# Other queues for the stores, other places in memory and another order at two seams of a diffusion layer

## The chip, the cores and the metric

The kernel runs on one core of a Trainium2 chip. Its engines are TensorE (PE, matmuls), VectorE (DVE), ScalarE (ACT), GpSimd (POOL) and SyncE (SP), which here only issues DMAs. Each engine runs its own instructions in order, and waits on semaphores for the others. The metric is the device time of one execution in microseconds (us), lower is better; three runs of the kernel before gave a median of 2388.57 (2385.91 to 2389.51).

## The reference

One layer over 2048 tokens of width 1024 with 256 context tokens: a bidirectional gated linear attention (GLA) and a SwiGLU with hidden width 2816, each between two RMS norms and modulated by a conditioning vector. Cut to what is run:

```python
h_lat = modulate(rms_norm(lat, g0), m0, m1)
y_lat, _ = gla_mixer(h_lat, h_ctx, ...)        # chunk scans in both directions, head norm, silu(r), w_out
lat = lat + m2 * rms_norm(y_lat, g1)
h = modulate(rms_norm(lat, g2), m3, m4)
gate, up = jnp.split(h @ ffn_w_in, 2, axis=-1)
lat = lat + m5 * rms_norm((jax.nn.silu(gate) * up) @ ffn_w_out, g3)
```

## The kernel before

All matmuls are done in three passes on split operands (`hi` is rounded to fp32r, `lo` is the rest: hi x hi, hi x lo, lo x hi). The program is written as stages, and a scheduler of the framework puts each engine's instructions in an order of its own; what it may do is set by the memory pools. A pool takes a place on the left or right side of SBUF or PSUM, its tiles have a number of buffers (`bufs`), and a tile of a later pool that lies over an earlier one waits for that pool's close and for the tiles there (`reuse_waits="tile"`).

The first stage makes the projections, gates and the chunks' scores. The second is the back pass (`back`, L654 to 757): chunk after chunk, from 15 to 0, the state E is taken along, `o` is formed (L695), normed (`on`, L703, by POOL's `rh`), gated and transposed, and projected by `wo` (`py`, L739, whose squares ACT sums). With POOL's `ry` DVE scales it (L751), adds the residual `xt` (L753, on POOL but for the last chunk), SP stores the sum `l1_d` (`l_d` in the trace, L754), and a norm (`xh`, L93 and L95, by POOL's `rb`) follows. `mh`, `my`, `mb` and `sst` are the small sums ahead of `rh`, `ry` and `rb`.

SwiGLU's input is the modulated transpose of `xh` (L102/103). It is multiplied by a seven-product scheme of the Strassen kind: each half `p` of the tokens needs seven operands T_d[p][P1..P7]. Two are the transposes of a group of 512 tokens (`first`); the other five come from the other group (`second`, L771 to 787): two loads `bl`, two transposes `hf`, four differences (L781) and their stores. POOL forms them for the group that comes first, DVE for the last group (group 0), whose units stand as `pend` behind the back pass. Each T is loaded and split by `load_T` (L855 to 863) into a pool that is partly (`hR`) only opened when the back pass's right side (`p2t`) has closed.

SwiGLU (L897 to 990) runs 44 features, 2 halves of the tokens by 22 pieces. `Feat.product(i)` splits a weight block (`whl`, L933/934) and does twelve matmuls of 128x512 into X, Y or Z; the products come in the order `CHAIN`, P1, P2, P6, P7, P5, P4, P3. The results `a` are stored, with differences `sa`, into S_d; sums of the second weight matrix (`wl`) are stored into W_d in between. The last stage (`out_group`) multiplies S_d by W_d or the weights through rings `ar`, `wr` and `wraw` (L1026 to 1039), fourteen deep, and ends with a norm (L1052 to 1056). All stores are issued by SP (`st` is `nc.sync`).

Of the kernel before, what the change touches and what calls it, by code (L numbers as in the profile page):

```python
# [15 lines left out]
D = 1024  # L16
# [3 lines left out]
H = 4  # L20
# [14 lines left out]
def trunk(ctx, tc, x, cx, modw, cols, rows, consts, wqkr, wv, wvg, wgate, wout, w1, w2, out):  # L35
# [17 lines left out]
    qb_d = [dram.tile([128, H, 128], F32, name=f"qb_d{c}") for c in range(NC_)]  # L53

# [12 lines left out]
    pT = ExitStack()  # L67
    tbp = pT.enter_context(tc.tile_pool(name="tbp", bufs=1))
    Tb = tbp.tile([128, H, DV], F32, name="Tb")
# [105 lines left out]
    Tf = gp.tile([128, H, DV], F32, name="Tf")  # L175
    glt = [c1.tile([128, 128], F32R, name=f"glt{i}") for i in range(4)]
# [177 lines left out]
    def gla_stages(g, i, c, first):  # L354
# [279 lines left out]
    p2t = ExitStack()  # L634
    sp = p2.enter_context(tc.tile_pool(name="sp", bufs=2, reuse_waits="tile"))
# [14 lines left out]
    def back(gc):  # L650
# [13 lines left out]
        def b0():  # L664
# [10 lines left out]
            if gc == NC_ - 1:  # L675
                E[0] = sp.tile([128, H, DV], F32, name="E", tag="E", bufs=3)
                for h in range(H):
                    nc.scalar.activation(out=E[0][:, h, :], in_=Tb[:, h, :], func=AF.Copy, scale=fb[:, gc, h:h + 1])
# [50 lines left out]
        def b3(n):  # L729
            ohi, olo = e["o"]  # L730
            if n == 0:
                e["y"] = sq.tile([128, D], F32, name="y2", tag="y2", bufs=2)
# [9 lines left out]
        def b4(xhs):  # L742
# [11 lines left out]
            st.dma_start(out=l1_d[gc], in_=y)  # L754
# [4 lines left out]
    def h2_units(g, xhs):  # L759
# [3 lines left out]
        def hmod(k):  # L763
            hf = sq.tile([128, GT], F32, name="hf2", tag="hf2", bufs=4)
# [6 lines left out]
        def second(k):  # L771
# [6 lines left out]
            st.dma_start(out=Td[P3][k], in_=b22)  # L778

            def comb(i, out, x, y):  # L780
                eng.tensor_tensor(out=out, in0=x, in1=y, op=ALU.subtract)  # L781
                st.dma_start(out=Td[i][k], in_=out)
# [3 lines left out]
            t2 = sq.tile([128, GT], F32, name="t2", tag="hf2", bufs=4)  # L786
# [5 lines left out]
        return [lambda k=k: second(k) for k in range(4)]  # L792

# [29 lines left out]
    for i, gc in enumerate(order):  # L823
# [12 lines left out]
        if gc % 4 == 0:  # L836
            pend += h2_units(gc // 4, xhs[gc // 4][::-1])
    p2.close()
    pT.close()
# [3 lines left out]
    p3 = ExitStack()  # L843
    hL = p3.enter_context(tc.tile_pool(name="hL", bufs=1, reuse_waits="tile"))
    w3 = p3.enter_context(tc.tile_pool(name="w3", bufs=2, reuse_waits="tile"))
    o3 = p3.enter_context(tc.tile_pool(name="o3", bufs=2, reuse_waits="tile"))
    ps3 = p3.enter_context(tc.tile_pool(name="ps3", bufs=1, space=PSUM, reuse_waits="tile"))
    for u in pend:
        u()
    p2t.close()  # L850
    hR = p3.enter_context(tc.tile_pool(name="hR", bufs=1, reuse_waits="tile", side="right"))
    ps3z = p3.enter_context(tc.tile_pool(name="ps3z", bufs=1, space=PSUM, reuse_waits="tile", side="right"))
    T = {}

# [42 lines left out]
    class Feat:  # L897
# [32 lines left out]
        def product(self, i):  # L930
# [6 lines left out]
            if i == P1:  # L937
                self.X = ps3.tile([128, GT], F32, name="X", tag="X", bufs=3)
# [56 lines left out]
    for i in CHAIN:  # L995
        load_T(1, i)
# [193 lines left out]
```

## Time and profile before

| | value |
|---|---|
| profiled execution | 2384.77 us |
| its span | 2383.0 us (1.8 around it) |
| median of three runs | 2388.57 us (2385.91 to 2389.51) |
| mean granted PE clock | 0.986 of full speed |
| busy share | PE 97%, DVE 65%, ACT 45%, POOL 8% |
| DMA | 463.98 MB, mean 195 GB/s |

The table is read so: PE's 97% is an average; 3% of the span, some 81 us, is PE idle time, and a transfer or another engine that PE waits for shows as a gap of its timeline, with what released it in brackets. In PE rows "x12" groups matmuls of one kind, and the next start minus this start is what they take. `SPq` is the DMA queue of SP: a row is the issue of a transfer, not its landing.

### The profile page before, as it was taken

Reading aid. Unit: us, or ns where it says so; the run is one execution under the profiler, and the core shown is the slowest. Engines: PE = TensorE matmul, PEld = TensorE weight load, DVE = VectorE, ACT = ScalarE, POOL = GpSimd, SP = SyncE. Lnnn points to the kernel's source line nnn. Section 1 sums busy time; section 2 is a strip of 40 time slices with the busy share of each in tenths; the row PEclk is TensorE's granted clock in tenths of the full one; section 3 lists DMA queues with packets and bytes.
Section 4 is the critical chain, followed back from the end, with each engine's and each line's share of the span. In section 5 each row is a group of like instructions: output and inputs, shape, how many; then the busy total and the mean of one; then the engine's idle time right before and its main releaser. Section 6 shows DMA issues by size and latency. Waiting matters only on the chain.

```text
span 2383.0 us, 32426 instructions
## 1 busy us (share of the span) xinstructions
PE 2302.0 (97%) x11546; PEld 1939.9 (81%) x11546; DVE 1557.7 (65%) x2478; ACT 1068.8 (45%) x1947; POOL 186.6 (8%) x274
## 2 busy tenths in 40 slices
PE   8999999999998999897999999999999989999998
PEld 4898898898898878685888888888888868888887
DVE  6756666766658576658776666866666647466554
ACT  3535445445547544335433333533333336554552
POOL 1100000000001033631000000000000000001001
PEclk9999999999999999997999999999999999999999
DMA  8765468565455587758787332633233248559655
GB/s 299 225 208 173 148 197 285 177 210 208 153 191 191 206 274 257 243 186 309 258 264 259 125 111 93 230 102 115 97 106 107 75 149 284 191 192 330 201 181 177
DMA packets 228902, 463.98 MB, mean 195 GB/s; under 512 B 22530, under 2 KB 66178, under 8 KB 228740
## 3 DMA queue, kind: packets, MB, share of 16 engines
q1 hardware_dynamic: 228740, 461.92, 57.3%
q8 instruction: 90, 1.47, 0.3%
q14 instruction: 72, 0.59, 0.1%
HBM read 331.27 MB, written 130.56 MB: 194 GB/s over the span
## 4 chain that ended last, share of the span: by engine, by line
PE 52%; DMA 0%; DVE 0%; SPq 0%; ACT 0%; issue 0%; POOLq 0%; POOL 0%; ACTq 0%
PE X L951 20%; PE Z L951 10%; PE X L1074 10%; PE W L1074 8%; PE Y L951 5%; DMA wraw<-w 0%; DMA T<-T_d 0%; DMA T_d<-hf 0%; DVE sa L984 0%; DVE bl L781 0%; DVE y L1055 0%; SPq L906 0%; DVE t L781 0%; DVE hf L781 0%; DVE a L974 0%
## 5 line engine op out<-in xcount | busy, mean ns | idle before, releaser
L951 PE MATMUL X<-T,whl 128*128 128x512 f32 x2112 | 495.7, 390 | 8.2 <-ACT whl L933 7.1
L951 PEld LDWEIGHTS X<-T,whl 128*128 128x128 f32 x2112 | 396.6, 188 | 91.5 <-ACT whl L933 7.5
L951 PE MATMUL Z<-T,whl 128*128 128x512 f32 x1056 | 256.2, 391 | 9.1 <-ACT T L861 9.1
L1074 PE MATMUL X<-wr,ar 128*128 128x512 f32 x1056 | 242.3, 391 | 10.6 <-ACT wr L1038 10.6
L1074 PEld LDWEIGHTS X<-wr,ar 128*128 128x128 f32 x1056 | 199.2, 189 | 52.8 <-ACT wr L1038 11.1
L951 PEld LDWEIGHTS Z<-T,whl 128*128 128x128 f32 x1056 | 199.3, 189 | 51.6 <-ACT T L861 9.5
L86 PE MATMUL pj<-hhi,whi 128*128 128x512 f32 (+1 forms) x544 | 213.6, 395 | 2.1 <-DVE hhi L75 1.4
L87 PE MATMUL pj<-hlo,whi 128*128 128x512 f32 (+1 forms) x544 | 211.4, 389 | 0.0
L88 PE MATMUL pj<-hhi,wlo 128*128 128x512 f32 (+1 forms) x544 | 210.4, 387 | 0.0
L73 ACT CAST whi<-wf 128x1024 fp32r<-128x1024 f32 x104 | 109.0, 1048 | 192.7 <-PE pj L87 84.4
L1028 DVE TENSOR_TENSOR ar<-ar 128x512 fp32r<-128x512 f32 x154 | 106.2, 691 | 131.1 <-ACT ar L1027 130.6
L76 DVE TENSOR_TENSOR wlo<-wf,whi 128x1024 fp32r<-128x1024 f32 x104 | 126.8, 1220 | 86.5 <-ACT whi L73 81.0
L1074 PE MATMUL W<-wr,ar 128*128 128x512 f32 x792 | 180.5, 389 | 0.0
L1074 PEld LDWEIGHTS W<-wr,ar 128*128 128x128 f32 x792 | 148.7, 188 | 30.8
L1027 ACT CAST ar<-ar 128x512 fp32r<-128x512 f32 x154 | 95.5, 621 | 154.6 <-DMA ar<-S_d 107.0
L86 PE MATMUL pj<-whi,hhi 128*128 128x256 f32 x432 | 125.0, 289 | 6.3 <-DVE gs L292 4.9
L951 PE MATMUL Y<-T,whl 128*128 128x512 f32 x528 | 127.7, 390 | 0.0
L87 PE MATMUL pj<-wlo,hhi 128*128 128x256 f32 x432 | 123.2, 285 | 2.8 <-DVE wlo L76 2.8
L88 PE MATMUL pj<-whi,hlo 128*128 128x256 f32 x432 | 122.7, 284 | 0.0
L87 PEld LDWEIGHTS pj<-hlo,whi 128*128 128x128 f32 x544 | 103.5, 190 | 21.3 <-DVE hlo L76 2.2
L86 PEld LDWEIGHTS pj<-hhi,whi 128*128 128x128 f32 x544 | 103.1, 191 | 21.5 <-DVE hhi L75 1.6
L88 PEld LDWEIGHTS pj<-hhi,wlo 128*128 128x128 f32 x544 | 103.4, 190 | 19.7
(231 smaller groups left out, 4273.7 us busy)
## 6 DMA issues: line engine op xcount, KB each, us to landing
ar<-S_d SPq DMA_DIRECT2D x154, 256.0 KB, 3.0
wf<-wqkr SPq DMA_DIRECT2D x68, 512.0 KB, 3.9
wg<-w SPq DMA_DIRECT2D x44, 512.0 KB, 3.5
wu<-w SPq DMA_DIRECT2D x88, 256.0 KB, 2.7
S_d<-sa SPq DMA_DIRECT2D x88, 256.0 KB, 2.0
wr<-W_d SPq DMA_DIRECT2D x88, 256.0 KB, 3.0
wf<-wv SPq DMA_DIRECT2D x36, 512.0 KB, 3.8
wl<-w SPq DMA_DIRECT2D x66, 256.0 KB, 3.7
```

Source lines behind the costliest of these rows:

```text
L73: nc.scalar.copy(out=hi, in_=src)
L76: nc.vector.tensor_sub(out=lo, in0=src, in1=hi.bitcast(F32))
L86: nc.tensor.matmul(out=ps, lhsT=ahi, rhs=bhi, start=start, stop=False)
L87: nc.tensor.matmul(out=ps, lhsT=ahi, rhs=blo, start=False, stop=False)
L88: nc.tensor.matmul(out=ps, lhsT=alo, rhs=bhi, start=False, stop=stop)
L951: nc.tensor.matmul(out=ps, lhsT=w[:, a, ks], rhs=t[:, k, b, :], start=first and k == 0 and n == 0, stop=k == 3 and n == 2, skip_group_chec ...
L1027: nc.scalar.copy(out=t[:, 0, :], in_=raw)
L1028: nc.vector.tensor_sub(out=t[:, 1, :], in0=raw, in1=t[:, 0, :].bitcast(F32))
L1074: nc.tensor.matmul(out=po[j], lhsT=a[:, x, 128 * j:128 * j + 128], rhs=w[:, z, :], start=first and fp == 0 and n == 0, stop=fp == NFP - 1 ...
```

## The change

Six things are changed. The stores of l1, of most operand sums, of W_d and of S_d are issued by `nc.gpsimd` (POOL) instead of SP: 250 DMA issues in all (only the P3 store for the first group stays on SP). The backward start state Tb is scaled in the first stage, stored and loaded back by a DMA, so that its memory ends early. T for P1 has a pool `hG` of its own, opened before the back pass, and is loaded when chunk 3 has been done; P2, P6, P7, P5 and P4 lie in `hL` on the left, and only P3, `wl`, `g1` and `sa` lie in `hR`. The first products are written in another order, with one unit of sums behind each of feature 0's P6, P7, P5 and P4. X has two PSUM buffers instead of three, Z one instead of two; `hf2` has three instead of four. And the last stage's rings are divided over three pools, of which `rA` (four of `ar`) and `rB` (ten of `wr`, `wraw`) lie over memory that frees early.

```diff
+                        for h in range(H):
+                            nc.scalar.activation(out=Tb[:, h, :], in_=Tb[:, h, :], func=AF.Copy, scale=fb[:, gc, h:h + 1])
+                        st.dma_start(out=Tb_d, in_=Tb.rearrange("p h v -> p (h v)"))
...
+    p3 = ExitStack()
+    hG = p3.enter_context(tc.tile_pool(name="hG", bufs=1, reuse_waits="tile"))
...
-                for h in range(H):
-                    nc.scalar.activation(out=E[0][:, h, :], in_=Tb[:, h, :], func=AF.Copy, scale=fb[:, gc, h:h + 1])
+                sync.dma_start(out=E[0].rearrange("p h v -> p (h v)"), in_=Tb_d)
...
-            st.dma_start(out=l1_d[gc], in_=y)
+            nc.gpsimd.dma_start(out=l1_d[gc], in_=y)
...
-            st.dma_start(out=Td[P3][k], in_=b22)
+            (st if g > 1 else nc.gpsimd).dma_start(out=Td[P3][k], in_=b22)
...
-                st.dma_start(out=Td[i][k], in_=out)
+                nc.gpsimd.dma_start(out=Td[i][k], in_=out)
...
-            t2 = sq.tile([128, GT], F32, name="t2", tag="hf2", bufs=4)
+            t2 = sq.tile([128, GT], F32, name="t2", tag="hf2", bufs=3)
...
+    T, T_pool = {}, {P1: hG}
+    def load_T(p, i):
+        t = T_pool[i].tile([128, 4, 2, GT], F32R, name=f"T{i}", tag=f"T{i}", bufs=1)
+        for k in range(4):
+            raw = t[:, k, 1, :].bitcast(F32)
+            sync.dma_start(out=raw, in_=T_d[p][i][k])
+            nc.scalar.copy(out=t[:, k, 0, :], in_=raw)
+            nc.vector.tensor_sub(out=t[:, k, 1, :], in0=raw, in1=t[:, k, 0, :].bitcast(F32))
+        T[i] = t
...
+        if gc == 3:
+            load_T(1, P1)
...
-    pT.close()
-    p3 = ExitStack()
+    w3 = p3.enter_context(tc.tile_pool(name="w3", bufs=2, reuse_waits="tile"))
...
-    w3 = p3.enter_context(tc.tile_pool(name="w3", bufs=2, reuse_waits="tile"))
...
-    for u in pend:
-        u()
-    p2t.close()
-    hR = p3.enter_context(tc.tile_pool(name="hR", bufs=1, reuse_waits="tile", side="right"))
-    ps3z = p3.enter_context(tc.tile_pool(name="ps3z", bufs=1, space=PSUM, reuse_waits="tile", side="right"))
-    T = {}
-    def load_T(p, i):
-        pool = hL if i in (P1, P2, P6) else hR
-        t = pool.tile([128, 4, 2, GT], F32R, name=f"T{i}", tag=f"T{i}", bufs=1)
-        for k in range(4):
-            raw = t[:, k, 1, :].bitcast(F32)
-            sync.dma_start(out=raw, in_=T_d[p][i][k])
-            nc.scalar.copy(out=t[:, k, 0, :], in_=raw)
-            nc.vector.tensor_sub(out=t[:, k, 1, :], in0=raw, in1=t[:, k, 0, :].bitcast(F32))
-        T[i] = t
+    T_pool.update({i: hL for i in (P2, P6, P7, P5, P4)})
...
-            t = o3.tile([128, 512], F32, name="wl", tag="wl", bufs=3)
+            t = hR.tile([128, 512], F32, name="wl", tag="wl", bufs=3)
...
-            st.dma_start(out=W_d[i][fp], in_=x)
+            nc.gpsimd.dma_start(out=W_d[i][fp], in_=x)
...
-                self.X = ps3.tile([128, GT], F32, name="X", tag="X", bufs=3)
+                self.X = ps3.tile([128, GT], F32, name="X", tag="X", bufs=2)
...
-                self.Z = ps3z.tile([128, GT], F32, name="Z", tag="Z", bufs=2)
+                self.Z = ps3.tile([128, GT], F32, name="Z", tag="Z", bufs=1)
...
-                g1 = o3.tile([128, GT], F32, name="g1", tag="g1", bufs=1)
+                g1 = hR.tile([128, GT], F32, name="g1", tag="g1", bufs=1)
...
-            st.dma_start(out=S_d[self.p][i][self.f % NFP], in_=t)
+            nc.gpsimd.dma_start(out=S_d[self.p][i][self.f % NFP], in_=t)
...
-                t = o3.tile([128, GT], F32, name="sa", tag="sa", bufs=3)
+                t = hR.tile([128, GT], F32, name="sa", tag="sa", bufs=3)
...
-    feats = {}
-    for i in CHAIN:
+    n = len(seq)
+    feats = {0: Feat(*seq[0]), 1: Feat(*seq[1])}
+    for i in (P2, P6, P7, P5, P4):
...
-    n = len(seq)
-    for t in range(n + 1):
+    for j, i in ((0, P1), (1, P1), (0, P2), (1, P2)):
+        feats[j].product(i)
+    for i in (P6, P7, P5, P4):
+        feats[0].product(i)
+        pend.pop(0)()
+    p2t.close()
+    hR = p3.enter_context(tc.tile_pool(name="hR", bufs=1, reuse_waits="tile", side="right"))
+    T_pool[P3] = hR
+    load_T(1, P3)
+    for j, i in ((1, P6), (0, P3), (1, P7)):
+        feats[j].product(i)
+    for _ in range(2):
+        units.pop(0)()
+    for t in range(2, n + 1):
...
-            if not 0 <= j < n:
+            if not j < n:
...
-        if t >= 2 and t % 2 == 0:
+        if t % 2 == 0:
...
-    r4 = p4.enter_context(tc.tile_pool(name="r4", bufs=1, reuse_waits="tile"))
+    rA = p4.enter_context(tc.tile_pool(name="rA", bufs=1, reuse_waits="tile"))
...
-    ps4 = p4.enter_context(tc.tile_pool(name="ps4", bufs=1, space=PSUM, reuse_waits="tile"))
+    rB = p4.enter_context(tc.tile_pool(name="rB", bufs=1, reuse_waits="tile"))
+    rC = p4.enter_context(tc.tile_pool(name="rC", bufs=1, reuse_waits="tile"))
+    ps4 = {"W": p4.enter_context(tc.tile_pool(name="ps4", bufs=1, space=PSUM, reuse_waits="tile")),
+           "X": p4.enter_context(tc.tile_pool(name="ps4x", bufs=1, space=PSUM, reuse_waits="tile", side="right"))}
+    count = {"ar": 0, "wr": 0}
+    def slot(tag):
+        i = count[tag] % 14
+        count[tag] += 1
+        first, nf = {"ar": (rA, 4), "wr": (rB, 10)}[tag]
+        pool, sfx, nb = (first, "", nf) if i < nf else (rC, "2", 14 - nf)
+        return pool.tile([128, 2, 512], F32R, name=tag, tag=tag + sfx, bufs=nb)
...
-        t = r4.tile([128, 2, 512], F32R, name=tag, tag=tag, bufs=14)
+        t = slot(tag)
```

The instructions are otherwise the same and as many. What the scheduler makes of it follows for three places.

PE at the seam from the back pass to SwiGLU, before (`py` is the last chunk's projection, the transposes `tp` are those of the last group's `xh`; T_10939 is P1's operand, T_10952 P2's, T_10965 P6's, T_10978 P7's):

```order
L88 MATMUL py<-wo_hi_8573,olo 128x512
L951 MATMUL X<-T_10939,whl 128x512 x2
L951 MATMUL Y<-T_10952,whl 128x512 x2
L951 MATMUL X<-T_10939,whl 128x512 x3
L102 MATMUL tp<-ident,xh 128x128 x24
L951 MATMUL X<-T_10939,whl 128x512 x4
L102 MATMUL tp<-ident,xh 128x128 x4
L951 MATMUL X<-T_10939,whl 128x512 x3
L951 MATMUL Y<-T_10952,whl 128x512 x4
L102 MATMUL tp<-ident,xh 128x128 x4
L951 MATMUL Y<-T_10952,whl 128x512 x6
L951 MATMUL X<-T_10965,whl 128x512 x12
```

and now (T_10487 is P1's, T_10854 P2's, T_10867 P6's, T_10880 P7's, T_10893 P5's and T_10906 P4's):

```order
L86 MATMUL py<-wo_hi_8579,olo 128x512
L951 MATMUL X<-T_10487,whl 128x512 x24
L100 MATMUL tp<-ident,xh 128x128 x24
L951 MATMUL Y<-T_10854,whl 128x512 x12
L951 MATMUL X<-T_10867,whl 128x512
L100 MATMUL tp<-ident,xh 128x128 x4
L951 MATMUL X<-T_10867,whl 128x512 x6
L951 MATMUL Y<-T_10854,whl 128x512 x12
L951 MATMUL X<-T_10867,whl 128x512 x5
L951 MATMUL Z<-T_10880,whl 128x512 x12
L951 MATMUL X<-T_10893,whl 128x512 x12
```

Both first features' P1 now stand in front of the transposes, and the products that follow come in the order in which the operands load. P3's first matmul stands 156 matmuls and 32 transposes behind `py`.

POOL in the sums of the first group, before, up to the next chunk's `rh` (`bl`, `hf` and `t` are the sums, y a chunk's residual sum):

```order
L781 TENSOR_TENSOR bl<-hf_10030,bl 128x512
L781 TENSOR_TENSOR hf_10030<-hf_10037,hf_10030 128x512
L781 TENSOR_TENSOR t_10049<-hf_10037,bl 128x512
L781 TENSOR_TENSOR bl<-bl,t_10049 128x512
L80 TENSOR_SCALAR mh<-ssh 128x4
L82 TENSOR_TENSOR rh<-mh,nhalf 128x4
L753 TENSOR_TENSOR y_9890<-y_9890,xt_10054 128x1024
L747 TENSOR_TENSOR sst<-ss_10075 128x1
```

and now:

```order
L784 TENSOR_TENSOR hf_10036<-hf_10043,hf_10036 128x512
L784 TENSOR_TENSOR t_10055<-hf_10043,bl 128x512
L785 DMA T_d_91<-hf_10036 128x512
L785 DMA T_d_90<-t_10055 128x512
L784 TENSOR_TENSOR bl<-bl,t_10055 128x512
L785 DMA T_d_88<-bl 128x512
L756 TENSOR_TENSOR y_9896<-y_9896,xt_10060 128x1024
L757 DMA l_d_119<-y_9896 128x1024
L78 TENSOR_SCALAR mb<-ss 128x1
L80 TENSOR_TENSOR rb<-mb,nhalf 128x1
L78 TENSOR_SCALAR mh<-ssh 128x4
L80 TENSOR_TENSOR rh<-mh,nhalf 128x4
```

Each sum has its store behind it on POOL, and y's sum, its store, `mb` and `rb` stand ahead of `mh` and `rh`; before, SP issued the stores, and y's sum stood behind `rh`.

SP at the end of SwiGLU, before (S_d stores, then the last stage's loads):

```order
L979 DMA S_d_95<-a_17496 128x512
L979 DMA S_d_96<-sa 128x512
L979 DMA S_d_97<-sa 128x512
L979 DMA S_d_94<-sa 128x512
L1021 DMA A_17582<-A_d_190 128x1024
L1026 DMA ar<-S_d_99 128x512
L1036 DMA wraw<-w 128x512
L1026 DMA ar<-S_d_99 128x512
L1036 DMA wraw<-w 128x512
```

and now:

```order
L903 DMA wg<-w 128x1024
L906 DMA wu_17368<-w 128x512
L906 DMA wu_17369<-w 128x512
L903 DMA wg<-w 128x1024
L1051 DMA ar<-S_d_99 128x512 x4
L1046 DMA A_17594<-A_d_191 128x1024
L1061 DMA wraw<-w 128x512 x4
L1077 DMA l_19005<-l_d_121 128x1024
L1051 DMA ar<-S_d_99 128x512
```

The stores are gone from the queue: four loads of `ar` and of `wraw` stand directly behind the last weights `wg`.

## Rows read from the trace of the kernel before

**Rows 1.** The page, busy us of each engine, share of the span, instructions.

```profile
PE 2302.0 (97%) x11546; PEld 1939.9 (81%) x11546; DVE 1557.7 (65%) x2478; ACT 1068.8 (45%) x1947; POOL 186.6 (8%) x274
```

**Rows 2.** Timeline of PE in mid-SwiGLU: start, us, engine line op, count.

```profile
1503.79 2.88 PE L951 MATMUL Y<-T,whl 128*128 128x512 f32 x12
1506.51 2.88 PE L951 MATMUL Z<-T,whl 128*128 128x512 f32 x12
```

**Rows 3.** Timeline of PE at seam 1; in brackets idle time and releaser.

```profile
1085.76 1.22 PE L951 MATMUL X<-T,whl 128*128 128x512 f32 x2 [7.09 <-ACT whl L933]
...
1091.13 4.67 PE L102 MATMUL tp<-ident,xh 128*128 128x128 f32 x24 [0.52 <-DVE xh L95]
...
1117.86 5.21 PE L951 MATMUL Z<-T,whl 128*128 128x512 f32 x12 [9.08 <-ACT T L861]
```

**Rows 4.** Windows of seam 1: length, each engine's busy time (count), clock, DMA.

```profile
1078.70:1117.80 39.10, 21.38 (x92) 17.09 (x92) 31.18 (x49) 19.01 (x34) 4.91 (x7) 0.75 0.90 312
...
1078.70:1117.80 39.10, 5.87 (x32) 5.46 (x32) 0.75 0.90 312
```

**Rows 5.** Timeline of ACT at seam 1.

```profile
1078.65 2.68 ACT L861 CAST T<-T 128x512 fp32r<-128x512 f32 x5
1081.24 0.59 ACT L739 ACTIVATE y<-py 128x512 f32<-128x512 f32 x1
...
1117.19 0.62 ACT L861 CAST T<-T 128x512 fp32r<-128x512 f32 x1 [7.02 <-DMA T<-T_d]
```

**Rows 6.** Timeline of SP's queue at seam 1.

```profile
1110.86 0.32 SPq L782 DMA_DIRECT2D T_d<-bl  x1
...
1113.01 5.19 SPq L860 DMA_DIRECT2D T<-T_d  x10
```

**Rows 7.** Timelines of PE, DVE, ACT and SP's queue at seam 2.

```profile
1955.23 4.94 PE L1074 MATMUL X<-wr,ar 128*128 128x512 f32 x13 [10.64 <-ACT wr L1038]
...
1945.25 0.69 DVE L974 TENSOR_TENSOR a<-a,g 128x512 f32<-128x512 f32 x1 [1.93 <-ACT g L973]
...
1947.43 0.69 DVE L984 TENSOR_TENSOR sa<-a,sa 128x512 f32<-128x512 f32 x1
...
1944.62 0.60 ACT L973 ACTIVATE g<-X 128x512 f32<-128x512 f32 x1 [7.57 <-PE X L951]
...
1954.56 0.62 ACT L1038 CAST wr<-wraw 128x512 fp32r<-128x512 f32 x1 [0.16 <-DMA wraw<-w]
...
1949.06 0.41 SPq L1026 DMA_DIRECT2D ar<-S_d  x1
```

**Rows 8.** Timeline of POOL in the first group's sums, and their window (as 4).

```profile
972.22 0.69 POOL L82 TENSOR_TENSOR ry<-my,nhalf 128x1 f32<-128x1 f32 x1
972.72 1.31 POOL L781 TENSOR_TENSOR bl<-hf,bl 128x512 f32<-128x512 f32 x1
...
988.36 2.40 POOL L753 TENSOR_TENSOR y<-y,xt 128x1024 f32<-128x1024 f32 x1 [4.12 <-DMA xt<-x]
...
1003.82 1.62 POOL L781 TENSOR_TENSOR bl<-bl,t 128x512 f32<-128x512 f32 x1
1008.55 0.21 POOL L80 TENSOR_SCALAR mh<-ssh 128x4 f32<-128x4 f32 x1 [3.11 <-ACT on L700]
...
1009.99 2.34 POOL L753 TENSOR_TENSOR y<-y,xt 128x1024 f32<-128x1024 f32 x1
...
972.70:1010.00 37.30, 32.69 (x157) 26.10 (x155) 23.64 (x38) 13.62 (x34) 28.84 (x28) 1.00 0.77 267
```

**Rows 9.** Timelines of DVE and PE there.

```profile
971.73 1.14 DVE L703 TENSOR_SCALAR on<-op,rh 128x256 f32<-128x256 f32 x4 [0.91 <-POOL rh L82]
...
1010.01 3.25 DVE L703 TENSOR_SCALAR on<-op,rh 128x256 f32<-128x256 f32 x4 [0.91 <-POOL rh L82]
...
1012.62 1.61 PE L722 MATMUL tp<-ident,on 128*128 128x128 f32 x8 [2.54 <-DVE on L703]
```

**Rows 10.** The l1 store's instructions: ns min/median/max, first and last start.

```profile
L754 SPq DMA_DIRECT2D l_d<-y x16: 319/320/327, 864.8 to 1087.1; - x16
```

More of the change, by code (lines that the diff above doesn't have):

```diff
@@ L53, in trunk @@
     qb_d = [dram.tile([128, H, 128], F32, name=f"qb_d{c}") for c in range(NC_)]
+    Tb_d = dram.tile([128, D], F32, name="Tb_d")
     ident = cst.tile([128, 128], F32, name="ident")
@@ L66, in trunk @@
     fb = cst.tile([128, NC_, H], F32, name="fb")
-    pT = ExitStack()
-    tbp = pT.enter_context(tc.tile_pool(name="tbp", bufs=1))
-    Tb = tbp.tile([128, H, DV], F32, name="Tb")
     def split(src, hi, lo, e_hi="act"):
@@ L175, in trunk @@
     Tf = gp.tile([128, H, DV], F32, name="Tf")
+    Tb = gp.tile([128, H, DV], F32, name="Tb")
     glt = [c1.tile([128, 128], F32R, name=f"glt{i}") for i in range(4)]
@@ L731, in b3 @@
             if n == 0:
-                e["y"] = sq.tile([128, D], F32, name="y2", tag="y2", bufs=2)
+                e["y"] = c3.tile([128, D], F32, name="y2", tag="y2", bufs=2)
                 e["ss2"] = sq.tile([128, 2], F32, name="ss2", tag="ss2", bufs=2)
@@ L763, in hmod @@
         def hmod(k):
-            hf = sq.tile([128, GT], F32, name="hf2", tag="hf2", bufs=4)
+            hf = sq.tile([128, GT], F32, name="hf2", tag="hf2", bufs=3)
             transp_mod(ps2, "pa", 4, xhs, k, hf, mcol[:, 2, 1, k:k + 1], mcol[:, 2, 0, k:k + 1])
@@ L814, in trunk @@
     sq = p2t.enter_context(tc.tile_pool(name="sq", bufs=2, reuse_waits="tile", side="right"))
+    c3 = p2.enter_context(tc.tile_pool(name="c3", bufs=1, reuse_waits="tile"))
     c2b = p2.enter_context(tc.tile_pool(name="c2b", bufs=1, reuse_waits="tile", side="right"))
@@ L817, in trunk @@
     load_wo(range(4, KT), c2b, sq)
-    A2 = sq.tile([128, D], F32, name="A2", tag="A2", bufs=1)
+    A2 = c3.tile([128, D], F32, name="A2", tag="A2", bufs=1)
     sync.dma_start(out=A2, in_=A_d[0].to_broadcast([128, D]))
@@ L1034, in w2_block @@
         half, nn = {P1: (0, 0), P2: (1, 0), P3: (1, 1)}[i]
-        raw = r4.tile([128, 512], F32, name="wraw", tag="wraw", bufs=4)
+        raw = rB.tile([128, 512], F32, name="wraw", tag="wraw", bufs=4)
         sync.dma_start(out=raw, in_=w2[fp + NFP * half, :, 512 * nn:512 * nn + 512])
-        t = r4.tile([128, 2, 512], F32R, name="wr", tag="wr", bufs=14)
+        t = slot("wr")
         nc.scalar.copy(out=t[:, 0, :], in_=raw)
@@ L1059, in out_group @@
         lo, hi = slice(0, 512), slice(512, 1024)
-        X = [ps4.tile([128, 512], F32, name="X4", tag=tx, bufs=4) for j in range(4)]
+        X = [ps4[tx].tile([128, 512], F32, name="X4", tag=tx, bufs=4) for j in range(4)]
         y0 = [y4.tile([128, D], F32, name="y0", tag="y0", bufs=6) for j in range(4)]
@@ L1067, in out_group @@
             if i in (P2, P7):
-                W = [ps4.tile([128, 512], F32, name="W4", tag=tw, bufs=4) for j in range(4)]
+                W = [ps4[tw].tile([128, 512], F32, name="W4", tag=tw, bufs=4) for j in range(4)]
             po = W if i in (P2, P7, P4) else X
```

## The prediction, on record before the changed kernel ran

> **What bounds the kernel now.** Read first the busy shares [rows 1]: TensorE (PE) works 2302.0 of the span's 2383.0 us, so all that a change of order, queues and memory can give back is 81 us of PE idling plus time in which PE ran slow. Then PE's own timeline in the middle of SwiGLU [rows 2]: one product of twelve 512-column matmuls starts 2.72 us after the one before (1506.51 - 1503.79), 0.2267 us per matmul, with no gap. The change leaves PE's order there alone, so this stretch moves by nothing as long as operands come in time. What is left are three places, where I read PE's gaps and then the queue that ended each.
>
> Seam 1, from the mixer's last output projection to SwiGLU [rows 3]: gaps of 7.09 us ahead of the first product, 0.52 ahead of the transposes and 9.08 ahead of the first Z product at 1117.86. The window [rows 4] holds 92 matmuls, 32 of them transposes, at a granted clock of 0.75, that is part of it at 1.2 instead of 2.4 GHz. From 1078.5 to 1117.86 are 39.4 us; 60 product matmuls need 60 x 0.2267 = 13.6, the transposes 5.9 [rows 4]; 19.9 are lost. The twelve Z matmuls then take 5.21 [rows 3] instead of 2.72, 2.5 more: 22.4 us.
>
> Two waits make it. The last chunk's y square on ACT stands behind five casts of T in one block of 2.68 us [rows 5], and its norm behind that. And SP stores the operand sums in order: its last store waits for DVE until 1110.86, and only then do T's loads go out, at 1113.01 [rows 6], since their memory is freed by the sums; 4.85 us later PE has them.
>
> Seam 2, from SwiGLU to the output product [rows 7]: DVE's last difference ends at 1947.43 + 0.69 = 1948.12, SP waits for it to store it, and the first load of ar stands behind that at 1949.06; the cast follows at 1954.56 and PE starts at 1955.23 after 10.64 us. Its first 13 matmuls take 4.94 where 2.95 are due. 12.6 us lost.
>
> The third place is POOL's stretch of sums in the back pass [rows 8]: 28.84 of 37.3 us busy, the sums 1.31 to 1.62 us each, and PE waits behind it for 2.54 us at 1012.62 [rows 9].
>
> **The change part by part.** *Early loads at seam 1.* T for P1 lies in memory that is free early and is loaded three chunks before; both first P1 products (24 matmuls, 5.44 us) stand ready, and by the order they follow at 1078.5 at once. The norm's chain gets shorter: ahead of the last y square ACT has an xh and three casts instead of xh and five, 0.6 us less, and a DVE subtraction of 0.7 that had been in front of y's sum goes; the transposes come at 1089.8 instead of 1091.13. PE idles 1089.8 - 1083.9 = 5.9 there. Behind them stand four units of sums. Before, they took from 1091.13 to 1110.86, 19.7 us [rows 3, 6]; now their stores are POOL's, where POOL has nothing else, and add some 0.8 of delay at the end: 1110.3. But DVE must now split five T tiles (20 subtractions, at 0.73 us from start to start, as between 1945.25 and 1947.43 in [rows 7], 14.6 in all) in this same stretch, where before they lay ahead of it; DVE is busy 31.18 of 39.1 us there [rows 4], of its 7.9 idle I take 3.1 as usable, a choice: 11.5 later. Then the store lands (4.2, by the T load from its issue at 1113.01 to its cast at 1117.19, [rows 5, 6]), P3's T is loaded now that its memory is free, and is on PE 4.85 us later: 1110.3 + 11.5 + 4.2 + 4.85 = 1130.8. By the order 156 matmuls and 32 transposes precede P3: 1078.5 + 35.4 + 5.9 = 1119.8. So 11.0 are lost, with a slow clock as before (2.5) 13.5. Gain 22.4 - 13.5 = 8.9. Bounds: DVE's splits all hidden by other work, 19.9; the loads of 5 MB, which go out behind SP's waits at about 1087 and need 3.4 us each MB at the 312 GB/s of [rows 4], holding back each product in turn, 0. I take 8.9, near the middle, as DVE is 80% busy there.
>
> *Rings ahead of the end at seam 2.* Four ar and four wraw loads stand on SP before the end, ar's casts too; no store stands before them. Left after the last SwiGLU matmul are ACT's silu (0.60) and wr's cast (0.62), and on DVE a product and three differences until 1948.12 before wr's low part: the first matmul starts at about 1946, the second at 1948.9 [rows 7]. PE idles some 4.0 and loses up to 2 by the clock as before; I take 4.8 lost. 12.6 - 4.8 = 7.8, bounds 5 (a fifth DVE step or a late load) and 10 (all low parts in time).
>
> *POOL in the sums' zone.* Between the first sum and the end of rh, 972.72 to 1009.99, POOL now also issues 16 stores of sums and two of l1, 18 in all. No row shows what POOL pays for one. Bounds: SP's own issue of the same store, 0.32 us [rows 10]; POOL's passes over such a tile, 1.31 to 1.62 [rows 8]. I take 0.7, by POOL's instruction with hardly any data (ry, 0.69, [rows 8]). Before, 7.2 of the 37.3 us were waits: 4.12 for xt, which SP loaded behind stores that waited for POOL, and 3.11 for ACT [rows 8]. Without them 30.1; y's sum and rb now stand ahead of mh (2.34, and 0.9 by mh's 0.21 and ry's 0.69, 3.2); 18 x 0.7 = 12.6. Together 45.9, 8.6 over. Against this, the DVE scaling of `on` took 3.25 us beside POOL's y sum and 1.14 away from it [rows 9]; in the new order they no longer meet, and 1.6 comes back (2.1 less what now meets a store). **+7.0**, as PE waits for `on`; bounds +0.2 at 0.32 and +23.6 at 1.62.
>
> That POOL and DVE hold each other up is what these two rows of `on` show. The Trainium skill (SBUF — State Buffer, section "SBUF: two separate sides") speaks against the change here: a DMA issued by POOL has its descriptors written by GpSimd, which is locked out while DVE runs certain two-port instructions, so that such a transfer appears blocked. No run yet shows it for a store. By that rule the stores would cost more in this zone than POOL's bare time and the sum would move toward +23.6. DMA: Bandwidth & Descriptors (the Trainium skill, "Specifications") gives about 1 us to the first byte on that path against 0.6 on SP's; taken as an estimate of the store's cost, the zone would cost +12.4 and the total be -4.3.
>
> *The rest at nothing.* 44 stores of W_d and 154 of S_d go to POOL, which has no other work in SwiGLU's 820 us; PE's unbroken row [rows 2] hides them, and without that cover a slot that comes free late costs a product a part of a store's 0.7. X has two buffers instead of three and Z one instead of two: by PE's order one product (2.72 us) stands between X's last matmul and the first on its other use, two stand between Z's, and a reader takes 0.6 to 0.7 [rows 7]; no wait. The backward state is scaled earlier and comes by a load: -2.4 if four ACT passes of 0.6 were in PE's way, +4.85 if the load is late; 0, since the load goes out ahead of its use.
>
> Sum: -8.9 - 7.8 + 7.0 = -9.7 on the profiled execution's 2384.77: 2375.1. The median of the timed runs is 2388.57, 3.8 above it; so 2378.9, **2379**.
>
> **The rivals.** *Cheap stores:* at 0.32 the zone costs 0.2 and 16.5 are gained: 2372. For it: POOL's share is 8% [rows 1]. *Costlier stores, no change:* at 1.0, halfway between ry's 0.69 and a sum's 1.31, the zone costs 12.4, the sum is -4.3: 2384. *Seam 1 not won:* T's loads and the single DVE queue hold each first product, gain 0, and -7.8 + 7.0 leaves -0.8: 2388. For it speaks DVE's 80% and a DMA share of 0.90 in the window [rows 4]; against it, that 24 matmuls stand ready. *POOL becomes the bound, slower:* each store takes POOL as long as a sum beside DVE, 1.62; in the sums' zone 18 x 1.62 = 29.2, the zone +23.6 and the total +6.9: 2395. It decides from 1.24 us a store (no gain) and is slower by over 0.2% from 1.51. For it the 3.25 of `on` [rows 9]; the rule of SBUF — State Buffer (the Trainium skill, section as above) would lead to it. Against it, that a store does no arithmetic on the tile.
>
> **How the numbers follow.** 0.2% is 4.8 us, about what timing this kernel can tell from nothing (the runs lie 3.6 apart). Forecast 0.40, cheap stores 0.18, no change by stores at 1.0 us 0.14, seam 1 not won 0.12, slower 0.16. Faster 0.40 + 0.18 - 0.01 (the forecast's own edge) = 0.57, same 0.14 + 0.12 + 0.01 = 0.27, slower 0.16. The range: the cheap case a little lower, 2369, up to 2394, just short of POOL as the bound. The forecast's own range, with a store between 0.5 and 0.9 and seam 1's gain between 5 and 13, is 2371 to 2387.
>
> **What would show it.** Right: PE's row begins X x24 at the end of the last py without a gap, then one gap of about 6 us before the transposes; the gap at seam 2 falls from 10.64 to about 4, ended by DVE's wr; POOL's sums spread with gaps of about 0.7; PE's waits between 972 and 1020 grow by about 7 in all. Wrong: stores that hold POOL for over 1.2 us or less than 0.4; waits of PE inside SwiGLU on Z, X or wg; PE waiting at P2, P6, P7 in turn for T; a wait on E at the start of the back pass. Nothing in the trace of before says how the clock will be granted at the shorter gaps; were it full there, some 4 us more would be won.

## The result: slower by 1.31%

The changed kernel took 2420.82 us (2416.15 to 2421.96), the kernel before 2389.04 on the same chip: ratio 1.0131, 95% interval 1.0114 to 1.0149. The prediction, 2379, was wrong in sign. The profiled execution took 2420.76 us, 36.0 more than that of before. To see where, take the same PE instruction in both traces (every 48th `py` matmul, the first of a Y product, and so on) and follow how far it is behind.

| PE reaches | before | after | behind | forecast |
|---|---|---|---|---|
| `py` of the eighth chunk | 939.34 | 947.34 | +8.0 | 0 |
| `py` of the tenth | 969.71 | 984.40 | +14.7 | 0 |
| `py` of the 13th, behind the sums on POOL | 1022.48 | 1043.85 | +21.4 | +7.0 |
| first Z product, P3's wait still to come | 1117.86 | 1131.27 | +13.4 | not stated |
| fifth Y product, behind seam 1 | 1180.11 | 1195.64 | +15.5 | -1.9 |
| 13th Y product | 1332.42 | 1370.94 | +38.5 | -1.9 |
| last stage's first W block, behind seam 2 | 1986.99 | 2018.96 | +32.0 | -9.7 |
| its last X block | 2346.03 | 2381.36 | +35.3 | -9.7 |

The three places of the forecast came out near its numbers, seam 1 least: POOL's sums +6.7 (7.0 forecast), seam 1 -5.9 to the fifth Y product (-8.9; it is -8.3 at the first Z, but P3's wait, the largest loss of the forecast's sum, comes behind that), seam 2 -6.5 (-7.8). The loss is what had been costed at nothing: 23.0 us in SwiGLU's early features, 14.7 ahead of the sums, 3.3 in the last stage. Each trace is one execution: in two other kernels with PE's order of before (only S_d's stores on POOL, without and with the rings of the change) the tenth chunk's `py` comes 2.0 and 1.2 us later than in the trace of before, so that much of the 14.7 need not be the change's.

Seam 1 in PE's timeline after (start, us, engine, line, op, count, idle before); it answers to [rows 3]:

```profile
1100.18 2.93 PE L951 MATMUL X<-T,whl 128*128 128x512 f32 x12
1107.38 4.61 PE L951 MATMUL X<-T,whl 128*128 128x512 f32 x12 [4.27 <-DVE y L754]
1112.01 2.85 PE L100 MATMUL tp<-ident,xh 128*128 128x128 f32 x24
...
1122.72 0.79 PE L951 MATMUL X<-T,whl 128*128 128x512 f32 x1 [2.99 <-ACT T L804]
...
1131.27 2.88 PE L951 MATMUL Z<-T,whl 128*128 128x512 f32 x12
...
1156.32 1.93 PE L951 MATMUL X<-T,whl 128*128 128x512 f32 x6 [2.57 <-ACT T L804]
```

The 9.08 us for T are gone. Only the first of the two P1 products runs at once; the second waits until DVE has read the last `py` (y, L754), which the forecast didn't see. P3 comes 56 us behind the last `py` (forecast 52). Seam 2, PE and then SP's queue, against [rows 7]:

```profile
1984.29 0.50 PE L1099 MATMUL X<-wr,ar 128*128 128x512 f32 x1 [1.19 <-ACT wr L1063]
1987.29 8.10 PE L1099 MATMUL X<-wr,ar 128*128 128x512 f32 x27 [2.50 <-DVE wr L1064]
...
1959.53 0.99 SPq L1051 DMA_DIRECT2D ar<-S_d  x2
...
1964.09 1.76 SPq L1061 DMA_DIRECT2D wraw<-w  x4
```

The two gaps are 3.69 us where 10.64 stood and 4.0 were forecast. What POOL pays for a store: its groups, the W_d stores' durations in ns (min/median/max), and the median us from issue to landing of the same stores, from POOL and then, in the kernel before, from SP:

```profile
L979 POOL DMA_DIRECT2D S_d<-sa x88 | 47.6, 541 | 149.0 <-DVE sa L984 144.7 <-DVE s L922 3.2 <-issue 0.9
L757 POOL DMA_DIRECT2D l_d<-y x16 | 10.0, 627 | 8.6 <-POOL y L756 4.5 <-DVE y L756 4.1
...
L875 POOL DMA_DIRECT2D W_d<-wl x44: 539/540/544, 1161.4 to 1342.0; - x44
...
S_d<-sa POOLq DMA_DIRECT2D x88, 256.0 KB, 2.3
S_d<-a POOLq DMA_DIRECT2D x66, 256.0 KB, 3.4
W_d<-wl POOLq DMA_DIRECT2D x44, 256.0 KB, 4.0
l_d<-y POOLq DMA_DIRECT2D x16, 512.0 KB, 5.5
```

```profile
S_d<-sa SPq DMA_DIRECT2D x88, 256.0 KB, 2.0
S_d<-a SPq DMA_DIRECT2D x66, 256.0 KB, 2.1
W_d<-wl SPq DMA_DIRECT2D x44, 256.0 KB, 2.9
l_d<-y SPq DMA_DIRECT2D x16, 512.0 KB, 3.1
```

So what a store costs POOL, unknown to the forecast, was 0.54 to 0.63 us (0.7 taken). But a store from POOL also landed later, by 0.3 us (`sa`), 1.1 (W_d), 1.3 (`a`) and 2.4 (l1), which no term had. In SwiGLU PE now waits:

```profile
1275.65 5.49 PE L951 MATMUL Z<-T,whl 128*128 128x512 f32 x12 [4.59 <-DVE a L968]
...
1321.42 5.17 PE L951 MATMUL Z<-T,whl 128*128 128x512 f32 x12 [4.49 <-DVE a L968]
```

### The profile page after: what moved, and what is told of

It reads as the page before. It is cut to its first block, busy times and chain, and to the rows that moved or that the text cites. A ratio compares the mean times of both kernels' runs of the same rounds, so it can differ in the third digit from the quotient of the medians.

```text
span 2419.0 us, 32537 instructions
## 1 busy us (share of the span) xinstructions
PE 2323.5 (96%) x11546; PEld 1947.8 (81%) x11546; DVE 1563.7 (65%) x2478; ACT 1066.6 (44%) x1947; POOL 322.7 (13%) x524
## 4 chain that ended last, share of the span: by engine, by line
PE 45%; issue 7%; POOL 4%; DMA 2%; DVE 2%; ACT 0%; POOLq 0%; DVEq 0%; ACTq 0%; SPq 0%
PE X L951 15%; PE X L1099 10%; PE Z L951 8%; PE W L1099 7%; PE Y L951 4%; DMA wl<-w 1%; POOL W_d L875 1%; POOL y L756 1%; POOL S_d L979 1%; POOL T_d L785 0%; DMA W_d<-wl 0%; PE py L84 0%; PE py L86 0%; PE py L85 0%; POOL bl L784 0%
```

## The experiments

All ratios are to the kernel before, with 95% intervals. Two theories for SwiGLU: Z's single bank lets DVE's lateness reach PE, or the W_d stores on POOL make DVE late.

**A second bank for Z.**

```diff
-                self.Z = ps3.tile([128, GT], F32, name="Z", tag="Z", bufs=1)
+                self.Z = zp[self.f // NFP].tile([128, GT], F32, name="Z", tag="Z", bufs=1)
```

(zp[0] is a pool on the right, opened with hR, for half of the features.)

> The changed kernel with a second PSUM bank for Z from the third feature on (even pieces' Z on the right side). In the changed kernel SwiGLU's first twelve features run 23 us later than their start (the second Y product is 15.5 us behind the kernel before, the product of feature 13 is 38.5 us behind), with PE waits of 0.6 to 4.6 us on Z for DVE's sum a+=Z. Theory one (Z's single bank lets DVE's waits for wl reach PE, which the second bank hid before): these 23 us go, 2420.8 becomes 2396 to 2403. Theory two (the W_d stores issued by POOL make wl's slots come free later and DVE itself falls behind): the waits move to X or whl and at most 5 us go, 2415 to 2421.

Measured 2415.83, ratio 1.0113 (1.0096 to 1.0130). Theory one fails: only 5 us go, and the waits move to X (0.97, 5.25 and 4.96 us for DVE's a+=X).

**W_d's stores on SP.**

```diff
-            nc.gpsimd.dma_start(out=W_d[i][fp], in_=x)
+            st.dma_start(out=W_d[i][fp], in_=x)
```

> The changed kernel with the 44 stores of W_d issued by SP again, all else as changed; PE's order is the same. Theory one (Z's single bank): DVE still waits for wl, as in the kernel before (37.5 us of waits there, 58.6 in the changed one), and PE with it: 2413 to 2421. Theory two (POOL's store in wl's loop, 0.54 us of POOL and a landing of 3.5 us): the 23 us go, 2395 to 2402.

Measured 2401.38, ratio 1.0057 (1.0035 to 1.0079): 19 us of 32 come from these 44 stores. With one bank of Z still, PE waits nowhere for a+=Z.

**l1 and the sums on SP; then all stores on SP.** The same edit on `l1_d` and `Td`; then on `W_d` and `S_d` too.

> The changed kernel with the stores of l1 and of the operand sums issued by SP again. The changed kernel's output projections of chunks 8 to 12 run from 8 to 22 us behind the kernel before. Theory one (18 stores of 0.55 us, with 0.3 us of waiting before most, delay rh and so on): 10 to 14 us go, 2407 to 2411. Rival (the transposes, the order and the loads of that stretch are what is late, not POOL): under 4 us go. The stretch before chunk 8 (7 us late from the first chunk on) stays late by both.

Measured 2404.24, ratio 1.0066 (1.0045 to 1.0087): 16.6 us go, more than either expected. In the trace the first Z product comes 16.0 us earlier, and the stretch from the fifth to the 13th Y product loses 14.2 us instead of 23.0.

> The changed kernel with every store issued by SP, as before: what is left is the memory, the order of the first products, one bank of Z and the backward state through memory. Theory one (POOL costs 10 to 14 us in the sums, Z's bank 23): 2407 to 2411, plus up to 6 where the last stage's first loads stand behind S_d's stores again: 2407 to 2417. Theory two (POOL's stores cost both): 2385 to 2392.

Measured 2387.47, ratio 0.9999 (0.9987 to 1.0011). Theory two's number: all 33 us come with the stores' queue (the scheduler then also moves 94 of PE's matmuls at seam 1). Memory and order without it are worth nothing in sum: in the trace the back pass ends 12.0 us behind the kernel before, and seam 1 gives back 12.6.

**Only the sums on SP, l1 on POOL.**

> The changed kernel with only the operand sums' stores issued by SP again; l1's, W_d's and S_d's stay on POOL. With l1's too on SP it gained 16.6 us (2404.2). Theory (the sums' stores stand between POOL's sums and rh, and at seam 1 each waits for DVE and lands late, while l1's store comes once a chunk): 12 to 16 us go, 2405 to 2409. Rival (l1's stores, ahead of mb, rb and rh in every chunk, are the cost): under 6 us go, 2415 to 2421.

Measured 2417.99, ratio 1.0121 (1.0106 to 1.0136), neither by itself. In the traces the first Z product comes at 1131.27 with both on POOL, 1122.76 with l1 alone, 1115.32 with none: the sums' stores cost 8.5 us up to there, l1's 7.4. Behind it the early features lost 5.6 us more than in the changed kernel, so the total hid it.

**The stores on POOL in the kernel before.**

> The kernel before with the same stores on POOL as in the changed one, memory and order of products as before. Theory one (POOL's stores cost what the undoing gave back: some 17 us in the sums and at seam 1, some 19 with W_d): slower by 20 to 36 us, less 3 to 7 that the free SP queue gives back at seam 2: 2405 to 2425. Rival (the stores cost only together with the changed memory, its three hf2 and one Z bank): slower by under 10 us: 2385 to 2398.

Measured 2415.28, ratio 1.0116 (1.0092 to 1.0140). The queue costs 27.6 us in the old memory and order, with two banks of Z and four hf2, nearly as much as the 33 in the new: theory one.

**Five slots of wl.**

```diff
-            t = hR.tile([128, 512], F32, name="wl", tag="wl", bufs=3)
+            t = hR.tile([128, 512], F32, name="wl", tag="wl", bufs=5)
```

> The changed kernel, its W_d stores on POOL still, with five buffers of wl instead of three (and seven of whl instead of eight, to make room). Theory one (a POOL store comes later and lands later, 4.0 us against 3.0 from SP, so wl's three slots come free too late and DVE waits for wl's loads, 58.6 us in the changed kernel, 28.5 with W_d on SP): with five slots DVE's wait for wl falls under 25 us, PE's waits on Z for a+=Z go, and 15 to 20 us go from 2420.8: 2400 to 2406. Rival (POOL's queue itself, in order behind S_d's stores, or the dense order of the sums on DVE is what is late): the waits stay, 2413 to 2421.

Measured 2426.81, ratio 1.0168 (1.0151 to 1.0184). My theory of slots fell: DVE's waits for wl went from 60.4 to 40.7 us, but with more slots the scheduler packs the 44 units into 128 us, and it got worse. The seven buffers of whl are a rival that this run doesn't part from the packing: another run with seven (the state in place, below) lost 5.8 us in this stretch with W_d on SP, where those with eight lost nothing. The packing led to the next.

**The units spread.** PE's order is the same.

```diff
-            units.pop(0)()
+            with tc.issue_after(feats[t].ld): units.pop(0)()
```

(feats[t].ld is the feature's wg load; SP queues the unit's loads behind it.)

> The changed kernel, stores on POOL, three slots of wl, one bank of Z: only the weight sums' loads are queued one unit behind each feature's wg load, so that the 44 units spread over SwiGLU instead of its first 180 us; PE's order is the same. With five slots the units came denser (127 us) and it got slower, so the theory is now: DVE works in order, and in the dense stretch its own work plus its waits for wl (58.6 us in 180 in the changed kernel, 28.5 in 175 with W_d on SP) exceed the time that PE leaves it. Spread, DVE has room: PE's waits for a+=Z of 14 us and the slow clock behind them go, and 17 to 23 us of 2420.8: 2398 to 2404. Rival (POOL's store itself holds DVE up, by its landing or by the shared access to memory, at any density): the waits stay in number and the time over 2413.

Measured 2398.81, ratio 1.0039 (1.0024 to 1.0054): 22 us go, the stores still on POOL. The windows show where. DVE's busy time is the third number pair, PE's the first, the clock behind the five pairs; for the stretch of the units: changed kernel, and the group of DVE's wl instructions there (busy, mean ns, idle before them):

```profile
1160.00:1342.00 182.00, 168.12 (x704) 136.10 (x704) 121.47 (x197) 55.52 (x99) 38.92 (x72) 0.95 0.73 244
...
L874 DVE TENSOR_TENSOR wl<-wl 128x512 f32<-128x512 f32 x44 | 30.4, 691 | 60.4 <-DMA wl<-w 58.6 <-issue 1.6
```

W_d on SP:

```profile
1158.00:1334.00 176.00, 176.00 (x777) 145.42 (x777) 134.80 (x218) 64.77 (x113) 18.38 (x34) 1.00 0.80 269
...
L874 DVE TENSOR_TENSOR wl<-wl 128x512 f32<-128x512 f32 x44 | 30.3, 690 | 36.3 <-DMA wl<-w 28.5 <-issue 5.4 <-DMA W_d<-wl 1.0
```

five slots:

```profile
1162.00:1290.00 128.00, 110.91 (x446) 88.58 (x444) 87.03 (x140) 35.37 (x63) 34.00 (x63) 0.92 0.88 301
...
L874 DVE TENSOR_TENSOR wl<-wl 128x512 f32<-128x512 f32 x44 | 30.3, 690 | 40.7 <-DMA wl<-w 40.4
```

and spread:

```profile
1160.00:1342.00 182.00, 182.00 (x803) 150.44 (x802) 122.49 (x194) 67.39 (x117) 26.50 (x49) 1.00 0.47 160
...
L874 DVE TENSOR_TENSOR wl<-wl 128x512 f32<-128x512 f32 x14 | 9.6, 686 | 6.8 <-DMA wl<-w 6.8
```

Add DVE's busy time to its waits for wl: 121.5 + 60.4 = 181.9 of 182 us in the changed kernel, 87.0 + 40.7 = 127.7 of 128 with five slots: DVE has no idle time but these waits, and PE loses 99 matmuls (803 - 704) against the spread order, 22 us, 14 of them idle and the rest at a lower clock (0.95 in the mean). With W_d on SP it is 171.1 of 176, spread 129.3 of 182: DVE has room and PE waits for nothing.

The sum alone doesn't tell a loss, though. The same two rows of the kernel before:

```profile
1130.00:1316.00 186.00, 186.00 (x822) 154.02 (x821) 140.15 (x229) 69.38 (x122) 0.00 (x0) 1.00 0.79 260
...
L874 DVE TENSOR_TENSOR wl<-wl 128x512 f32<-128x512 f32 x43 | 29.6, 689 | 42.0 <-DMA wl<-w 37.5 <-issue 2.4 <-DMA wu<-w 1.3
```

and of the kernel before with the stores on POOL:

```profile
1150.00:1330.00 180.00, 168.97 (x735) 138.48 (x733) 122.96 (x199) 58.00 (x104) 38.30 (x71) 0.98 0.71 238
...
L874 DVE TENSOR_TENSOR wl<-wl 128x512 f32<-128x512 f32 x41 | 28.4, 692 | 53.3 <-DMA wl<-w 50.9 <-DMA W_d<-wl 2.2
```

Both stand at 98%, 182.2 of 186 and 176.3 of 180 us, and PE works through in the first and idles 11 us in the second. What parts them is the waits for wl. In the nine traces with W_d's stores on SP, close together and with eight buffers of whl, they are 36.3 to 46.4 us in all, and PE loses nothing from the fifth to the 13th Y product; in the five with these stores on POOL they are 53.3 to 62.3, and PE loses 14.2 to 26.4. So a full DVE costs nothing by itself, but has nowhere to put a longer wait.

**The state through memory, alone, in the kernel before.** The diff's edits on Tb and E.

> The kernel before with the backward state scaled in the first stage, stored and loaded as E by a DMA, all else as before. Every version of the change so far has its first output projection 6.4 to 10.3 us behind the kernel before (838.1 to 842.1 against 831.8). Theory one (the state's way is what delays it, as o<-E,qb moves back by 16 projection matmuls on PE and the loads of qb stand behind it): the first projection at 838 to 842, the run 4 to 8 us slower, 2392 to 2396. Rival (the order there comes from the pools of the change, hG and the others): the first projection within 2 us of 831.8, the run as before, 2387 to 2390.

Measured 2394.14, ratio 1.0027 (1.0016 to 1.0038): +6.4 us; the first `py` starts at 840.27 instead of 831.77. One trace doesn't size that, as two other kernels with PE's order of before have the first `py` at 834.90 and 835.54; the timed runs do. PE's first o<-E moves behind 14 more projection matmuls, and SP's next qb load stands behind the stores of r; in the changed kernel (PE, then SP):

```profile
837.27 3.78 PE L698 MATMUL o<-E,qb 128*128 128x256 f32 x8 [2.93 <-DMA qb<-qb_d]
...
832.10 1.83 SPq L245 DMA_DIRECT2D r_d<-stg  x2
...
834.57 0.74 SPq L673 DMA_DIRECT2D qb<-qb_d  x1
```

**Seam 2 alone, in the kernel before:** S_d on POOL, then with the rings of the change too.

> The kernel before with only S_d's 154 stores on POOL. At seam 2 SP then waits for no store: the first ar load can go out when its memory is free, at 1944 to 1946 instead of 1949.1, so 3 to 5 of the 10.6 us go: 2383 to 2385. Rival (POOL's stores of S_d cost in SwiGLU, their landing 3.4 us instead of 2.1 holding up a and sa): 2388 or more.

Measured 2390.36, ratio 1.0007 (0.9997 to 1.0016): a miss. Without the rings SP's loads still go out late, with no store ahead of them (the first ar at 1953.80, PE idles 11.92 us): the queue alone doesn't shorten the gap.

> The kernel before with S_d's stores on POOL and the last stage's rings and PSUM pools as in the change. Seam 2 as in the change: PE's gap there 3.7 to 5 us instead of 10.6, so 6 to 8 us go; if the rings' place makes the last stage's blocks of 132 matmuls 30.1 to 30.3 us, 3.4 come back: 2383 to 2386, and without that 2380 to 2382.

Measured 2385.29, ratio 0.9984 (0.9975 to 0.9993). PE idles 3.69 us. The rings alone don't do it either: in the changed kernel with all stores on SP the loads of `wraw` stand behind S_d's last stores, and PE idles 7.75 us (PE, then SP):

```profile
1951.77 1.52 PE L1099 MATMUL X<-wr,ar 128*128 128x512 f32 x2 [7.75 <-ACT wr L1063]
...
1946.13 1.77 SPq L979 DMA_DIRECT2D S_d<-sa  x3
1948.01 2.19 SPq L1061 DMA_DIRECT2D wraw<-w  x4
```

So the gap of 10.64 us goes to 11.92 by the queue, to 7.75 by the rings and to 3.69 by both. And the last stage's blocks get slower. Before, then in the changed kernel:

```profile
1986.99 30.08 PE L1074 MATMUL W<-wr,ar 128*128 128x512 f32 x132
2016.91 30.08 PE L1074 MATMUL X<-wr,ar 128*128 128x512 f32 x132
```

```profile
2018.96 30.43 PE L1099 MATMUL W<-wr,ar 128*128 128x512 f32 x132
2049.23 30.43 PE L1099 MATMUL X<-wr,ar 128*128 128x512 f32 x132
```

From start to start 29.92 before and 30.27 now (30.03 to 30.27 for the blocks behind the first). S_d's stores on POOL alone leave 29.92, and the runs with the rings, with these stores on POOL or on SP, have 30.03 to 30.27: the rings or their PSUM pools make it. Two attempts to say which part:

```diff
-           "X": p4.enter_context(tc.tile_pool(name="ps4x", bufs=1, space=PSUM, reuse_waits="tile", side="right"))}
+           "X": None}; ps4["X"] = ps4["W"]
...
-        first, nf = {"ar": (rA, 4), "wr": (rB, 10)}[tag]
+        first, nf = {"ar": (rA, 4), "wr": (rB, 14)}[tag]
```

> The version with all stores on SP, with the last stage's PSUM tiles in one pool on the left as before. In every version of the change a block of 132 matmuls of the last stage takes 30.1 to 30.3 us instead of the even 29.92 of the kernel before, 3.4 us in all. If the place of the PSUM tiles makes it, the blocks return to 29.92; if the place of the rings in SBUF does, they stay at 30.1 to 30.3.

A single execution, 2393.3: blocks still 30.03 to 30.27, so not the PSUM pools.

> The kernel before with S_d on POOL and the last stage's rings as in the change, but with all fourteen wr buffers in one pool (rB) and only the ten later ar in rC. In the run before this one matmuls on some steps took 398 ns and on others 388. If the place of wr's last four buffers (in rC) makes it, the blocks of 132 return to 29.92 us and the time is 2381 to 2383; if the ar buffers in rC or their addresses make it, the blocks stay at 30.1 to 30.4 and the time at 2384 to 2387.

Measured 2386.87, ratio 1.0000 (0.9990 to 1.0010): still 30.03 to 30.27, so it isn't the place of wr's last four buffers. Why these matmuls are slower stays open.

**Putting the parts together.**

> The changed kernel with the stores of l1, the sums and W_d issued by SP, only S_d's by POOL, and a second bank for Z: what both theories leave as the good parts. With all stores on SP it took 2387.5, its last stage starting 9.5 us after SwiGLU's last product; with S_d on POOL that is 4 to 5 us; two waits on Z of 2 us in all go. Sum 2387.5 - 6 - 2 = 2379 to 2382, 0.25 to 0.4% below the kernel before. Rival (S_d's stores on POOL cost in SwiGLU too): 2385 to 2392.

Measured 2388.18, ratio 0.9997 (0.9986 to 1.0007): a miss. In its trace (2382.68, near the fastest of the ten) the back pass ends 10.9 us behind the kernel before, seam 1 gives 12.0, seam 2 5.4, and the last stage takes 3.5.

> The version with only S_d's stores on POOL and two banks for Z, in which the backward state also stays on chip: it is scaled in place and used as the first E (two more E buffers instead of three, seven of whl instead of eight, for the room). By the run in which the state's way through memory alone cost 0.27% (6.4 us): the first output projection returns to within 2 us of 831.8, and the time is 2388.2 - 6 = 2380 to 2384. Rival (the pools and the transposes' order cost the rest of the back pass, and fewer E and whl buffers cost as much): 2386 to 2392.

Measured 2391.10, ratio 1.0017 (1.0005 to 1.0029), a miss: the first `py` was at 830.56, but P3's T came 6.5 us late, and PE again waited for X. With the units spread besides it was 2387.29, ratio 0.9996 (0.9986 to 1.0005), where 2378 to 2382 was expected.

> The changed kernel with only S_d's stores on POOL, two banks of Z, the weight sums paced and wr's fourteen buffers together: the parts that gained, with the state still through memory (6.4 us). By the parts: 2388 before, seam 1 -11, seam 2 -6.5, state +6.4, the back pass's rest and SwiGLU's start +5, blocks 0 to +3.4: 2382 to 2386. Rival (what is won at seam 1 is given back as T for P3 comes late, as in the version with the state in place): 2386 to 2391.

Measured 2384.53, ratio 0.9990 (0.9980 to 0.9999), as expected. This and the rings with S_d's stores on POOL are the only versions whose interval lies below the kernel before, by 0.1 to 0.2%.

## Why the prediction was wrong

**Seams.** Seam 2 was right in mechanism and about in size, -6.5 for -7.8: the forecast took the queue and the memory as one, and the runs show that either alone doesn't shorten the gap to that (11.92 and 7.75 us, 3.69 with both). Seam 1 was right in kind and a third short, -5.9 for -8.9: the second P1 product didn't run at once but waited 4.27 us, and PE waited for T at P2 and P6 (0.84 and 2.99 us), one of the forecast's own signs of being wrong. With all stores on SP it gave 12.3 between the same points.

**POOL's sums.** +6.7 for +7.0, in the kernel before with POOL's stores +7.3 at the same place. The forecast's sum on POOL holds: from the first sum to the end of `rh` (987.70 to 1034.27) it took 46.6 us, 45.9 forecast; a store held POOL 0.54 to 0.63 us (once 0.94), and before eight of the 18 it waited 0.3 for the instruction ahead. But PE didn't pay "as PE waits for `on`". POOL's, DVE's, ACT's and PE's timelines of the changed kernel:

```profile
1008.44 1.03 POOL L80 TENSOR_TENSOR rh<-mh,nhalf 128x4 f32<-128x4 f32 x1
...
1009.51 1.14 DVE L706 TENSOR_SCALAR on<-op,rh 128x256 f32<-128x256 f32 x4 [5.59 <-POOL rh L80]
...
1016.72 0.78 ACT L101 ACTIVATE hf<-tp,mcol 128x512 f32<-128x512 f32 x1 [7.12 <-DMA T_d<-hf]
...
1017.55 2.07 PE L698 MATMUL o<-E,qb 128*128 128x256 f32 x4 [5.35 <-ACT hf L101]
```

and the waits in that stretch (us in total, times, longest), 970 to 1016 before, then 985 to 1035 after:

```profile
PE o L695 <- ACT hf L103: 4.6, 2, 3.2
PE tp L722 <- DVE on L703: 2.5, 1, 2.5
ACT hf L103 <- DMA T_d<-hf: 3.4, 1, 3.4
```

```profile
PE o L698 <- ACT hf L101: 9.2, 3, 5.4
PE tp L725 <- DVE on L706: 1.6, 1, 1.6
ACT hf L101 <- DMA T_d<-hf: 14.5, 4, 7.1
```

PE's waits for `on` fell; those for ACT's hf doubled, and ACT stood still until stores of hf had landed. The two longest of these waits ended with the landing of P3's stores, which stayed on SP (issued at 988.28 and 1011.06, landed 5.6 us later each). So the sum came out by another path than the forecast's, in part by luck, and what made those two stores late stays open.

**The step that failed: "The rest at nothing".** It read PE's unbroken row in mid-SwiGLU and let that hide 198 stores, pricing a late slot at "a part of a store's 0.7". The 44 W_d stores are not in mid-SwiGLU but in its first 180 us, in a loop of three slots (load, DVE, store, load), with DVE in order in the middle. A late slot there cost no part of a store's 0.7: the landing came 1.1 us later, DVE waited 18 us more for wl, and as it had no idle time left, PE lost 23.0 us in the trace. Put back on SP these stores gave 19.4 us of the timed runs, and spread out on POOL 22.0, with PE's order unchanged in both. The windows of before (DVE at 182 of 186 us with its waits) would have shown that a longer wait had nowhere to go; the prediction looked at DVE only at seam 1. Z's single bank, also "no wait", was worth 5 us. The state's load, "0, since the load goes out ahead of its use", cost 6.4: the load landed at 823.85, 0.7 us ahead of its user, but only as the scheduler had put 14 projection matmuls in front of that. 5.5 us between the eighth and the tenth chunk, ahead of the sums, stand in the version with all stores on SP and not in those made from the kernel before; whether three hf2 instead of four or the order makes them was not run.

**The rivals.** The slower rival had its sign right and its place wrong: the loss was not POOL's time. Over the run POOL is 13% busy; in the sums' zone it is busy 41.3 of 46.6 us, but no store took 1.2 us. The rule cited from the Trainium skill (SBUF — State Buffer, "SBUF: two separate sides"), that a DMA issued by POOL appears blocked while DVE runs certain two-port instructions, doesn't show in POOL's issues: the W_d stores took 539 to 544 ns each beside a DVE without idle time. Nor do their landings follow DVE's load: 4.0 us in the close order and 2.8 spread out, with DVE as busy in the same 182 us (121.5 and 122.5). No run tests the rule by itself. That the first byte comes later on POOL's path than on SP's, about 1 against 0.6 us (the Trainium skill, DMA: Bandwidth & Descriptors, "Specifications"), agrees in sign with all the landings above, and roughly in size with those of `sa` (2.3 against 2.0) and of W_d spread out (2.8 against 2.3); W_d's 1.1 in the close order is more.

## What to carry to other kernels

Price a store by its landing too, wherever its tile's slot is waited for: take the loop of load, work and store, and ask what an engine in order does with its wait. Before calling a stretch covered, add busy time and waits of each helper engine in it, in windows at the place where the moved work runs; an engine at 98% still covers what it did before, but not a longer wait. And when the work of such an engine stands close together in one stretch, try spreading it: here that gave as much as taking the stores back.

## What the hardware showed that was not expected

The same 132 matmuls took 29.92 us per block with one placing of their operand rings and 30.03 to 30.27 with another, no wait between them (389 ns each before; now 389 for two thirds and 392 to 398 for the rest); PSUM's place did not matter. The 44 issues of W_d's stores by POOL took 539 to 544 ns each, close together or spread out alike.
